# Every third lower weight part of the second block's projections, made by GpSimd

## The chip, the cores and the metric

The kernel runs on one core of one Trainium2 chip. The metric is the device time of one execution in microseconds (us). The core has five engines that each work through their own instructions in a fixed order: TensorE (PE in the rows; its weight loads are PEld), VectorE (DVE), ScalarE (ACT), GpSimd (POOL) and SyncE (SP, which issues the DMAs here). Engines wait for one another through semaphores. An instruction that waits holds up all that stand behind it on its engine.

## The reference

Two different transformer blocks run one after the other on 256 tokens of width 1024. The second one, cut to the part that matters here:

```python
c_q, c_kv, k_pe, dq, dk, dv = split(h @ w_in, [384, 256, 32, 512, 512, 512])
# _mla: 8 heads of 96 columns, the last 32 of them with rotary positions
q  = _rms(c_q, cq_g) @ w_uq
kv = _rms(c_kv, ckv_g) @ w_ukv              # 64 key and 64 value columns per head
q, k = _rms(q, q_g), _rms(concat(k_nope, k_pe), k_g)
o_mla = softmax(mask(q @ k.T * scale)) @ v
# _diff_attn: 4 heads, each with two softmaxes that are subtracted
o_diff = _rms((p1 - lam * p2) @ dv, subln_g) * (1.0 - lambda_init)
x = x + g1 * (concat(o_mla, o_diff) @ w_o)
x = x + g2 * _hmoe(h2, ...)                 # router and 16 experts
```

Everything is fp32. The first block (two feed-forward parts, token mixing, a per-layer embedding) and the experts of the second one are the larger share of the time. The change leaves both as they are.

## The kernel before

**Products.** TensorE multiplies in a reduced fp32 format, so every fp32 operand is split into an upper part `whi` and a lower part `wlo`, and a product takes three matmuls (`mm3`, L332 to L334). `split` (L336) makes the two parts: ScalarE copies the raw weights into the reduced format (L337), VectorE subtracts that from the raw weights (L338). The two lines are also used for activations (`xTh`, `xTl`, `cqTh`, `cqTl`).

**Pieces.** `piece` (L262) loads one piece of a weight matrix, at most 128 x 2048, with one DMA (L265) into a raw tile and cuts it into parts, of 128 x 512 as a rule, each with one split. There are three raw tiles in the stages spoken of here (`wraw`), which rotate: the DMA of a piece has to wait until all splits of the piece three before it have read their raw tile. SyncE issues these DMAs in program order, so one that waits holds back those behind it.

**The second block's projections.** `attention2` runs `mla_project` and `diff_project` interleaved. After the norm in front (around 1180 to 1200 us of the span) come, in the order of their DMAs: two pieces of the columns 0 to 672 of `w_in` (`lat`, the low-rank inputs), the V columns of `w_in`, `w_uq` in two pieces (queries, `mla_q`), `w_ukv` in two pieces (keys and values, `mla_k`), the columns 672 to 1696 of `w_in` in four pieces (`diff_q`, `diff_k`), and `w_o` in four pieces. For each query half and token tile there is a chain: matmuls into a bank `pj`, squares and sums (`gr_sq` L1338, `gr_ss` L1340), a reciprocal root (`rs_m`, `gr_rs`, L387 to L394), scaling (`mla_q` L1418, `mla_k` L1443), four transposes by TensorE (L1424, L1448) into `pt`, and a copy by ScalarE into `mla_qT` (L1428). Then scores and softmax follow (`mla_s` L1477).

**GpSimd** makes masks and position tables at the start. In the second block it only fills the two extra rows of the key and query tiles with mask constants: 16 instructions of 2 partitions for `mla_kT` (L1409) and 4 for `mla_qT` (L1427).

**Order.** A tile framework orders the instructions of each engine when the program is built, by priorities, and places the waits; the order is fixed when the program runs.

Of the kernel before, what the change touches and what calls it, by code (L numbers as in the profile page):

```python
# [8 lines left out]
F32 = mybir.dt.float32  # L9
# [3 lines left out]
ALU = mybir.AluOpType  # L13
# [39 lines left out]
class Net:  # L53
# [7 lines left out]
    hold = None  # L61
    first = ()
    log_behind = None

    def __init__(self, tc, ctx, a):
        self.tc, self.ctx, self.a = tc, ctx, a
        self.nc = tc.nc
        pool = lambda name, bufs, **kw: ctx.enter_context(tc.tile_pool(name=name, bufs=bufs, **kw))
        self.const = pool("const", 1)
        self.act = pool("act", 2)  # L70
        self.wraw = pool("wraw", 3)
        self.wspl = pool("wspl", 8)
        self.ring = pool("ring", 11)
        self.gring = pool("gring", 16)
        self.cring = pool("cring", 6)
        self.tmp = pool("tmp", 12)
        self.ps = pool("ps", 3, space=PSUM)
        self.psc = pool("psc", 3, space=PSUM)
        self.pst = pool("pst", 2, space=PSUM)
        self.tacts = []  # L80
        self.ada_part = []
        self.act_set(SILU_SET)
        self.masks()
# [172 lines left out]
    def piece(self, src, kk, n, by=0):  # L256

        nc = self.nc
        m = kk * n
        raw = self.raw()  # L260
        rv = raw[:, :m].rearrange("p (k n) -> p k n", k=kk)
        n0 = 0  # L262
        for z in src if isinstance(src, tuple) else (src,):
            n1 = n0 + z.shape[1]
            nc.sync.dma_start(out=rv[:, :, n0:n1], in_=z.rearrange("(k p) n -> p k n", p=P))  # L265
            n0 = n1
        k2, n2 = (min(kk, 1024 // n), n) if by == 0 else (kk, min(n, 1024 // kk))
        k2 = -(-kk // -(-kk // k2))
        out = []
        for k0 in range(0, kk, k2):  # L270
            for n0 in range(0, n, n2):
                h = rv[:, k0:min(k0 + k2, kk), n0:n0 + n2]
                w = h.shape[1]
                hi = self.wspl.tile([P, 1024], F32R, name="whi")[:, :w * n2].rearrange("p (k n) -> p k n", k=w)
                lo = self.wspl.tile([P, 1024], F32R, name="wlo")[:, :w * n2].rearrange("p (k n) -> p k n", k=w)
                cuts = [slice(None)]
                if w * n2 > 512 and (self.raws is None or self.raws <= 3):
                    cuts = [slice(0, w // 2), slice(w // 2, w)] if w > 1 else cuts
                for k in cuts:
                    ends = self.split(hi[:, k], lo[:, k], h[:, k])  # L280
                    for ins, o in zip(ends, self.before_weights):
                        self.after(ins, o)
                    if self.hold is not None:
                        self.after(ends[1], self.hold)
                    for ins, o in zip(ends, self.first):
                        self.after(ins, o)
                out.append((hi, lo))
        self.before_weights = ()
        return out
# [43 lines left out]
        mm(out, l[0], r[1], start=False, stop=False)  # L333
        mm(out, l[1], r[0], start=False, stop=stop)  # L334

    def split(self, hi, lo, src):  # L336
        h = self.split_hi = self.nc.scalar.activation(hi, src, AF.Copy).ins  # L337
        self.mark = self.nc.vector.tensor_tensor(lo, src, hi.bitcast(F32), ALU.subtract).ins  # L338
        return h, self.mark

# [1311 lines left out]
    def attention2(self):  # L1652
        nc, a = self.nc, self.a
        if self.depth == 0 or "p" not in self.stages:
            self.weave([self.attention_in(t) for t in range(NT)], 1)
        self.xT = self.hT
        oT = self.new_xT()
        m, d = self.mla_project(), self.diff_project()
        for n, z in enumerate((m, d, m, m)):
            self.weave(next(z))  # L1660
            if n == 1:
                self.first = ()
        mla = self.mla_attend(oT)
        self.weave(mla[0] + mla[1], 3)
        self.weave(next(d))
        diff = self.diff_attend(oT)
        self.weave(diff[0] + diff[1], 2)
        self.router_tables()
        self.router_weights()
        g1 = self.gate_row(0)  # L1670
        self.logits, self.xs, self.rt_rstd = {}, {}, {}
        self.rt_lg = self.c([P, NT, 20], "logits")
        w, o = a["w_o_2"][0], {}
        hs = lambda h: slice(h * 512, h * 512 + 512)
        pcs = {(h, k0): self.piece_k(w[k0 * P:k0 * P + 512, hs(h)], 4, 512) for k0 in (0, 4) for h in range(2)}

        def products(t, h, k0):

            if k0 == 0:
                o[t, h] = (self.ch_bank if t and h else self.mm_bank)("wo")  # L1680
            tt = slice(t * P, t * P + P)
            for k in range(k0, k0 + 4):
                self.mm3(o[t, h], (oT[0][:, k, tt], oT[1][:, k, tt]), pcs[h, k0][k - k0], k == 0, k == KD - 1)

        def finish(t, h):
            products(t, h, 4)
            r = self.s("wo_r")
            nc.vector.tensor_tensor(r, o[t, h], g1[h], ALU.mult)
            xs = self.x[:, t, hs(h)]
            self.summed = nc.vector.tensor_tensor(xs, xs, r, ALU.add).ins  # L1690
            self.router_in(t, h)
            if h == 1:
                rstd = self.rt_rstd[t] = self.c([P, 1], f"rt_rstd{t}")
                self.weave([self.rstd(rstd, self.mean_square(t), D)])
                nc.vector.scalar_tensor_tensor(self.rt_lg[:, t], self.logits[t][:, :20], rstd, self.rt_b, ALU.mult, ALU.add)
                self.tokens(t)

        for t, h in ((0, 0), (0, 1), (1, 0)):
            products(t, h, 0)
        finish(0, 0)  # L1700
        products(1, 1, 0)
        finish(0, 1)
        finish(1, 0)
        finish(1, 1)
# [239 lines left out]
    def moe(self):  # L1944
        nc, a = self.nc, self.a
        self.router()

        self.raws = 0

        def in_act():  # L1950
            z = self.new_xT()
            return lambda k: tuple(y[:, k:k + 2] for y in z)
        in_g = lambda k: tuple(self.g(n, F32R).rearrange("p (k n) -> p k n", k=2) for n in ("moe_xh", "moe_xl"))
        pair = lambda g, new: self.gather(2, lambda t: self.r1[:, t, g:g + 2], new)
        tiles = pair(0, in_act())
        self.act_set(SILU_SET, self.split_hi)
        self.g2 = self.gate_row(1)
        self.expert_tiles(tiles, [lambda name, e, g=g: a[name][0, g * E_PER_G + e] for g in range(N_GROUPS)], lambda: pair(2, in_g))

        v = nc.vector  # L1960
        info = self.c([1, 2], "over_f")
        ov = self.c([1, 4], "over_o")
        idx = self.c([1, 4], "over_i")
        for j in range(4):
            nc.gpsimd.memset(idx[:, j:j + 1], float(j * E_PER_G))
        v.tensor_reduce(info[:, 0:1], self.count[0:1], AX.X, ALU.max)
        v.tensor_scalar(ov, self.count[0:1], float(P), None, ALU.is_gt)
        v.tensor_tensor(ov, ov, idx, ALU.mult)
        v.tensor_reduce(info[:, 1:2], ov, AX.X, ALU.add)
        ii = self.c([1, 2], "over_ii", I32)  # L1970
        v.tensor_copy(ii, info)
        rr = self.c([P, NT], "over_r")
        v.tensor_reduce(rr, self.r1, AX.X, ALU.max)
        v.tensor_scalar(rr, rr, float(P), None, ALU.subtract)
        n = nc.values_load(ii[0:1, 0:1], min_val=0, max_val=S)
        e0 = nc.values_load(ii[0:1, 1:2], min_val=0, max_val=12)
        with self.tc.If(n > P):
            tiles = self.gather(1, lambda t: rr[:, t:t + 1], in_act())
            self.expert_tiles(tiles, [lambda name, e: a[name][0, bass.ds(e0 + e, 1)].rearrange("o k n -> (o k) n")])
# [85 lines left out]
```

## Time and profile before

| | |
|---|---|
| runs | 1656.74 us median of 3 (1653.23 to 1657.44) |
| profiled execution, its own time | 1653.4 us |
| its span | 1651.7 us, so 1.7 us lie around the span |
| PE busy | 1610.7 us (98%) |
| DVE busy | 1285.3 us (78%) |
| ACT busy | 896.4 us (54%) |
| POOL busy | 26.2 us (2%) |
| mean granted TensorE clock | 0.991 |

Times of single instructions below are microseconds from the start of the span. A busy share says how much of a stretch an engine had an instruction running, not how well it ran. The stage of the change lies between about 1180 and 1345 us; before it is the first block, after it the experts.

### The profile page before, as it was taken

To read this page: it belongs to the slowest core of one execution; us is meant where nothing else is said; L and a number is where in the kernel's file an instruction comes from. 1 tells how busy PE (TensorE), PEld (TensorE's weight loads), DVE (VectorE), ACT (ScalarE), POOL (GpSimd) and SP (SyncE) were. 2 spreads that over 40 slices of the span, in tenths; PEclk is the share of its full clock that TensorE was granted. 3 is DMA by queue.
4 is the path that set the end of the run, shared out by engine and by line. 5 is a ranking of instruction groups with operands and counts; after the bars stand their busy time and mean duration, and the time that the engine had idled before them with its cause. 6 is when DMAs were issued, how large, how long until landed. Compare 5 with 4: busy or idle time off the path is not lost.

```text
span 1651.7 us, 24570 instructions
## 1 busy us (share of the span) xinstructions
PE 1610.7 (98%) x9269; PEld 1344.7 (81%) x9269; DVE 1285.3 (78%) x2395; ACT 896.4 (54%) x1599; POOL 26.2 (2%) x90
## 2 busy tenths in 40 slices
PE   8999999999999999999999999999889999999998
PEld 6888898888888878888988888888778778787876
DVE  7668878577669886688885686697877769999896
ACT  6544365454553445544563645534475567777674
POOL 2000000000000000000000000000200000000000
PEclk9999999999999999999999999999999999999998
DMA  8667662236568756577532455676343239899995
GB/s 293 212 204 252 201 183 78 99 134 209 192 215 275 242 162 204 184 255 243 179 104 77 161 182 183 221 279 218 120 159 104 101 124 375 299 349 325 360 343 193
DMA packets 175261, 342.46 MB, mean 207 GB/s; under 512 B 13033, under 2 KB 49954, under 8 KB 175138
## 3 DMA queue, kind: packets, MB, share of 16 engines
q1 hardware_dynamic: 175138, 340.84, 60.4%
q8 instruction: 75, 1.23, 0.3%
q14 instruction: 48, 0.39, 0.1%
HBM read 339.76 MB, written 1.05 MB: 206 GB/s over the span
## 4 chain that ended last, share of the span: by engine, by line
PE 84%; DVE 9%; ACT 3%; DMA 2%; issue 1%; SPq 0%; DVEq 0%; ACTq 0%
PE gu L332 9%; PE gu L333 9%; PE gu L334 9%; PE pT L576 6%; PE y L334 4%; PE y L333 4%; PE y L332 4%; PE moe_h L333 4%; PE moe_h L334 3%; PE moe_h L332 3%; DVE wlo L338 2%; PE sc L576 2%; PE moe_y L333 2%; PE moe_y L332 2%; PE moe_y L334 2%; PE pj L332 2%
## 5 line engine op out<-in xcount | busy, mean ns | idle before, releaser
L338 DVE TENSOR_TENSOR wlo<-wraw,whi 128x512 fp32r<-128x512 f32 (+2 forms) x758 | 605.6, 831 | 157.2 <-ACT whi L337 155.0
L337 ACT ACTIVATE whi<-wraw 128x512 fp32r<-128x512 f32 (+2 forms) x758 | 528.3, 741 | 363.8 <-issue 104.2
L332 PE MATMUL gu<-whi,xTh 128*128 128x512 f32 (+1 forms) x736 | 274.9, 373 | 0.0
L333 PE MATMUL gu<-wlo,xTh 128*128 128x512 f32 (+1 forms) x736 | 274.1, 372 | 0.0
L334 PE MATMUL gu<-whi,xTl 128*128 128x512 f32 (+1 forms) x736 | 273.7, 372 | 0.0
L334 PEld LDWEIGHTS gu<-whi,xTl 128*128 128x128 f32 x736 | 138.8, 189 | 23.2
L332 PEld LDWEIGHTS gu<-whi,xTh 128*128 128x128 f32 x736 | 138.7, 188 | 23.1
L333 PEld LDWEIGHTS gu<-wlo,xTh 128*128 128x128 f32 x736 | 138.8, 189 | 22.7
L332 PE MATMUL y<-whi,hTh 128*128 128x512 f32 x224 | 87.7, 391 | 0.0
L334 PE MATMUL y<-whi,hTl 128*128 128x512 f32 x224 | 87.6, 391 | 0.0
L333 PE MATMUL y<-wlo,hTh 128*128 128x512 f32 x224 | 87.3, 390 | 0.2 <-DVE wlo L338 0.2
L332 PE MATMUL y<-whi,xTh 128*128 128x512 f32 x192 | 75.7, 394 | 0.0
L576 PE MATMUL pT<-xTh,whi 128*128 128x256 f32 x256 | 75.7, 296 | 0.0
L333 PE MATMUL y<-wlo,xTh 128*128 128x512 f32 x192 | 75.0, 391 | 0.0
L576 PE MATMUL pT<-xTl,whi 128*128 128x256 f32 x256 | 75.0, 293 | 0.0
L334 PE MATMUL y<-whi,xTl 128*128 128x512 f32 x192 | 75.0, 391 | 0.0
L576 PE MATMUL pT<-xTh,wlo 128*128 128x256 f32 x256 | 74.4, 291 | 0.0
L1166 DVE SCALAR_TENSOR_TENSOR ada<-ada_w,silu_c,ada 128x512 f32<-128x512 f32 x84 | 62.7, 746 | 12.7 <-DMA ada_w<-in_w_ada_dram 12.3
L1279 DVE SCALAR_TENSOR_TENSOR bias<-rel_m,rel_delta,bias 128x384 f32<-128x384 bf16 x116 | 63.9, 612 | 0.5
L109 ACT ACTIVATE ffn_h<-gu 128x512 f32<-128x512 f32 (+1 forms) x48 | 27.0, 563 | 55.4 <-PE gu L334 55.4
L337 ACT ACTIVATE xTh<-pt 128x512 fp32r<-128x512 f32 (+1 forms) x72 | 35.6, 500 | 35.1 <-PE pt L355 29.6
L333 PE MATMUL moe_h<-wlo,moe_xh 128*128 128x512 f32 x128 | 50.8, 397 | 1.7 <-DVE wlo L338 1.7
(570 smaller groups left out, 3254.6 us busy)
## 6 DMA issues: line engine op xcount, KB each, us to landing
wraw<-in_ffn_w_in_dram SPq DMA_DIRECT2D x88, 1024.0 KB
wraw<-in_ffn_w_out_dram SPq DMA_DIRECT2D x44, 1024.0 KB
wraw<-in_mix_w_in_dram SPq DMA_DIRECT2D x26, 1024.0 KB
ada_w<-in_w_ada_dram SPq DMA_DIRECT2D x96, 256.0 KB
wraw<-in_w_gate_dram SPq DMA_DIRECT2D x20, 1024.0 KB
wraw<-in_w_up_dram SPq DMA_DIRECT2D x19, 1024.0 KB
wraw<-in_w_down_dram SPq DMA_DIRECT2D x19, 1024.0 KB
wraw<-in_mix_w_out_dram SPq DMA_DIRECT2D x8, 1024.0 KB
```

The source lines that it names most:

```text
L109: ins = self.nc.scalar.activation(*args, **kw).ins
L332: mm(out, l[0], r[0], start=start, stop=False)
L333: mm(out, l[0], r[1], start=False, stop=False)
L334: mm(out, l[1], r[0], start=False, stop=stop)
L337: h = self.split_hi = self.nc.scalar.activation(hi, src, AF.Copy).ins
L338: self.mark = self.nc.vector.tensor_tensor(lo, src, hi.bitcast(F32), ALU.subtract).ins
L576: self.nc.tensor.matmul(o[:, :S], w[:, k], z[:, k], start=k == 0 and n == 0, stop=k == KD - 1 and n == 2)
L1166: z = nc.vector.scalar_tensor_tensor(acc, raw, c, acc, ALU.mult, ALU.add)
L1279: z = nc.vector.scalar_tensor_tensor(b, m, d, b, ALU.mult, ALU.add)
```

## The change

`piece` counts its splits (`turn`). While `share` is 3, every third split has its subtraction issued on GpSimd instead of VectorE. `share` is set to 3 in `attention2` ahead of the projections and back to 0 in front of the experts. The upper part stays on ScalarE. The other splits stay as they are. `mark`, which other code uses to put filler work behind the last subtraction, is not set by a GpSimd one.

```diff
     first = ()
     log_behind = None
+    turn = 0
+    share = 0
 ...
                 for k in cuts:
-                    ends = self.split(hi[:, k], lo[:, k], h[:, k])
+                    self.turn += 1
+                    ends = self.split(hi[:, k], lo[:, k], h[:, k], self.share and self.turn % self.share == 0)
 ...
-    def split(self, hi, lo, src):
+    def split(self, hi, lo, src, other=False):
+
         h = self.split_hi = self.nc.scalar.activation(hi, src, AF.Copy).ins
+        if other:
+            return h, self.nc.gpsimd.tensor_tensor(lo, src, hi.bitcast(F32), ALU.subtract).ins
         self.mark = self.nc.vector.tensor_tensor(lo, src, hi.bitcast(F32), ALU.subtract).ins
         return h, self.mark
 ...
         oT = self.new_xT()
+        self.share = 3
         m, d = self.mla_project(), self.diff_project()
 ...
         self.raws = 0
+        self.share = 0
```

What it does to the order of the instructions can be seen on three engines. Names with the same number are the same tile in both. Line numbers shift by a few: L265 becomes L267, L337 becomes L341, and those from L1224 on by six (L1409 becomes L1415, L1427 becomes L1433, L1428 becomes L1434, L1338 becomes L1344); GpSimd's subtraction is L343.

GpSimd from the last position table to the first instruction of the router, before:

```order
L1249 TENSOR_TENSOR rel_i_622<-pos_r_618,pos_nq_620 128x128
L1250 TENSOR_TENSOR rel_i_622<-pos_r_618,pos_nq_620 128x256
L1409 TENSOR_SCALAR mla_kT_11982<-early_137 2x2x64 x4
L1409 TENSOR_SCALAR mla_kT_11983<-early_137 2x2x64 x4
L1409 TENSOR_SCALAR mla_kT_11984<-early_137 2x2x64 x4
L1409 TENSOR_SCALAR mla_kT_11985<-early_137 2x2x64 x4
L1427 COPY mla_qT_12184<-early_137 2x512
L1427 COPY mla_qT_12187<-early_137 2x512
L1427 COPY mla_qT_12190<-early_137 2x512
L1427 COPY mla_qT_12193<-early_137 2x512
L1810 IOTA iota1i_12947 128x128
```

and now, from the last of the early subtractions on (11949 is of the V columns, 12006 and 12038 are `w_uq`, 12220 the second piece of `w_ukv`, 12498 and 12536 the first two pieces of the `diff` columns):

```order
L343 TENSOR_TENSOR wlo_11949<-wraw_11940,whi_11948 128x512
L343 TENSOR_TENSOR wlo_12015<-wraw_12006,whi_12014 128x384
L343 TENSOR_TENSOR wlo_12047<-wraw_12038,whi_12046 128x384
L343 TENSOR_TENSOR wlo_12223<-wraw_12220,whi_12222 128x512
L1415 TENSOR_SCALAR mla_kT_11982<-early_137 2x2x64 x4
L1415 TENSOR_SCALAR mla_kT_11983<-early_137 2x2x64 x4
L1415 TENSOR_SCALAR mla_kT_11984<-early_137 2x2x64 x4
L1415 TENSOR_SCALAR mla_kT_11985<-early_137 2x2x64 x4
L1433 COPY mla_qT_12184<-early_137 2x512
L1433 COPY mla_qT_12187<-early_137 2x512
L1433 COPY mla_qT_12190<-early_137 2x512
L1433 COPY mla_qT_12193<-early_137 2x512
...
L343 TENSOR_TENSOR wlo_12501<-wraw_12498,whi_12500 128x512
```

GpSimd has 19 subtractions more: 8 stand ahead of its twenty fills, 11 behind them (5 of the `diff` columns, 6 of `w_o`). Before, the fills stood behind nothing but the tables made at the start.

SyncE at the DMAs of the `diff` columns and the first two of `w_o`, with the engines that each waits for, before:

```order
L265 DMA wraw_12498<-in_w_in_2_dram 128x4x512 [waits DMAHW7_49,DVE_49]
L265 DMA wraw_12536<-in_w_in_2_dram 128x4x512 [waits DMAHW0_49,DVE_49,Activation_49]
L265 DMA wraw_12576<-in_w_in_2_dram 128x4x512 [waits DMAHW1_49,DVE_49,Activation_49]
L265 DMA wraw_12614<-in_w_in_2_dram 128x4x512 [waits DMAHW2_49,DVE_49,Activation_49]
L265 DMA wraw_12989<-in_w_o_2_dram 128x4x512 [waits DMAHW3_49,DVE_49]
```

and now:

```order
L267 DMA wraw_12498<-in_w_in_2_dram 128x4x512 [waits DMAHW7_49,DVE_49,Pool_49]
L267 DMA wraw_12536<-in_w_in_2_dram 128x4x512 [waits DMAHW0_49,DVE_49,Activation_49]
L267 DMA wraw_12576<-in_w_in_2_dram 128x4x512 [waits DVE_49,DMAHW1_49,Activation_49,Pool_49]
L267 DMA wraw_12614<-in_w_in_2_dram 128x4x512 [waits DVE_49,DMAHW2_49,Activation_49,Pool_49]
L267 DMA wraw_12989<-in_w_o_2_dram 128x4x512 [waits DMAHW3_49,DVE_49,Pool_49]
```

The order of the DMAs is the same. The fourth piece of the `diff` columns (12614) goes into the raw tile of the first one (12498), so it now waits for the subtraction `wlo_12501`, which stands behind all the fills on GpSimd.

ScalarE around the upper parts of that fourth piece, now:

```order
L341 ACTIVATE whi_12584<-wraw_12576 128x512 x2
L1434 ACTIVATE mla_qT_12184<-pt_12164,cols2_577 96x512
L341 ACTIVATE whi_12616<-wraw_12614 128x512 x2
L341 ACTIVATE whi_12622<-wraw_12614 128x512
L1434 ACTIVATE mla_qT_12187<-pt_12169,cols2_577 96x512
L341 ACTIVATE whi_12622<-wraw_12614 128x512
L1434 ACTIVATE mla_qT_12190<-pt_12174,cols2_577 96x512
L1344 ACTIVATE gr_sq_12242<-pj_12196 128x256
L1344 ACTIVATE gr_sq_12246<-pj_12197 128x256
L1344 ACTIVATE gr_sq_12250<-pj_12218 128x256
```

Before, the first upper part of 12614 stood ahead of `mla_qT_12184` and the other three between that and `mla_qT_12187`. The squares `gr_sq` begin the chain of the keys: their tile `pj_12196` is the first product with `w_ukv`. They stand behind all four upper parts of 12614.

## Rows read from the trace of the kernel before

**Rows 1.** The page: engines, and the chain that ended last, by engine.
```profile
PE 1610.7 (98%) x9269; PEld 1344.7 (81%) x9269; DVE 1285.3 (78%) x2395; ACT 896.4 (54%) x1599; POOL 26.2 (2%) x90
...
PE 84%; DVE 9%; ACT 3%; DMA 2%; issue 1%; SPq 0%; DVEq 0%; ACTq 0%
```

**Rows 2.** Stretch, its length, busy us of PE, PEld, DVE, ACT, POOL; clock, DMA share, GB/s.
```profile
1228.50:1246.30 17.80, 13.83 (x65) 10.11 (x64) 17.80 (x88) 13.14 (x41) 0.00 (x0) 1.00 0.60 193
1246.30:1281.00 34.70, 34.70 (x208) 29.26 (x208) 24.88 (x50) 19.74 (x59) 0.00 (x0) 1.00 0.33 106
```

**Rows 3.** Waits from 1228.5 to 1246.5: total us, times, longest us.
```profile
PE pj L332 <- DVE mla_q L1418: 2.1, 2, 1.3
...
PE pj L332 <- DVE rs_m L393: 1.6, 1, 1.6
```

**Rows 4.** GpSimd's groups in the whole span: busy us, mean ns, idle before.
```profile
L1427 POOL COPY mla_qT<-early 2x512 f32<-2x512 f32 x4 | 2.3, 613 | 17.6 <-PE pj L333 17.6
L1250 POOL TENSOR_TENSOR rel_i<-pos_r,pos_nq 128x256 int32<-128x256 int32 x1 | 0.6, 611 | 0.0
...
L204 POOL TENSOR_TENSOR m16f<-s,m4f 128x128 f32<-128x128 f32 x1 | 0.5, 452 | 0.1
...
L1249 POOL TENSOR_TENSOR rel_i<-pos_r,pos_nq 128x128 int32<-128x128 int32 x1 | 0.4, 398 | 38.1 <-DMA pos_r<-in_positions_dram 38.1
```

**Rows 5.** Timeline of GpSimd, 1165 to 1345: start, length, instructions, idle before.
```profile
1170.14 5.22 POOL L1409 TENSOR_SCALAR mla_kT<-early 2x128 f32<-2x128 f32 x8 [1118.79 <-DVE ln_r L417]
1185.60 7.63 POOL L1409 TENSOR_SCALAR mla_kT<-early 2x128 f32<-2x128 f32 x8 [10.23 <-ACT rms_h L1321]
1210.87 2.29 POOL L1427 COPY mla_qT<-early 2x512 f32<-2x512 f32 x4 [17.64 <-PE pj L333]
```

**Rows 6.** Timeline of SyncE's DMA issues, 1212 to 1240.
```profile
1217.38 14.14 SPq L265 DMA_DIRECT2D wraw<-in_w_in_dram  x4
1236.56 0.37 SPq L265 DMA_DIRECT2D wraw<-in_w_o_dram  x1
```

**Rows 7.** Timeline of ScalarE, 1218 to 1223, 1235 to 1243 and 1262 to 1272.
```profile
1220.98 1.67 ACT L337 ACTIVATE whi<-wraw 128x512 fp32r<-128x512 f32 x3
...
1236.46 0.63 ACT L337 ACTIVATE whi<-wraw 128x512 fp32r<-128x512 f32 x1 [1.66 <-DMA wraw<-in_w_in_dram]
...
1237.57 1.66 ACT L337 ACTIVATE whi<-wraw 128x512 fp32r<-128x512 f32 x3
1239.13 0.67 ACT L1428 ACTIVATE mla_qT<-pt,cols 96x512 f32<-96x512 f32 x1
...
1241.53 1.18 ACT L1338 ACTIVATE gr_sq<-pj 128x256 f32<-128x256 f32 x4
...
1268.80 1.15 ACT L337 ACTIVATE whi<-wraw 128x512 fp32r<-128x512 f32 x2 [2.69 <-PE pj L334]
```

**Rows 8.** Timeline of VectorE: around 1187, and 1221 to 1232.
```profile
1187.54 1.29 DVE L338 TENSOR_TENSOR xTl<-rms_h,xTh 128x512 fp32r<-128x512 f32 x2
...
1225.28 0.55 DVE L1340 TENSOR_REDUCE gr_ss<-gr_sq 128x4 f32<-128x384 f32 x1
...
1230.41 1.29 DVE L338 TENSOR_TENSOR wlo<-wraw,whi 128x512 fp32r<-128x512 f32 x2
```

**Rows 9.** Timeline of TensorE: first product with the `diff` columns, first transpose of keys.
```profile
1239.77 0.47 PE L332 MATMUL pj<-whi,xTh 128*128 128x512 f32 x1 [1.26 <-DVE mla_q L1418]
...
1246.38 0.61 PE L1448 MATMUL pt<-ident,mla_k 128*96 128x128 f32 x4
```

**Rows 10.** Timeline of GpSimd in two short windows, 1186.7 to 1187.5 and from 1190.5.
```profile
1186.19 3.02 POOL L1409 TENSOR_SCALAR mla_kT<-early 2x128 f32<-2x128 f32 x2
...
1190.54 0.53 POOL L1409 TENSOR_SCALAR mla_kT<-early 2x128 f32<-2x128 f32 x1
```

**Rows 11.** Busy time by stretch around TensorE's wait for the norm; columns as in rows 2.
```profile
1187.50:1192.50 5.00, 5.00 (x16) 5.00 (x17) 5.00 (x12) 3.91 (x6) 4.71 (x5) 0.50 0.00 0
1192.50:1203.00 10.50, 10.50 (x58) 9.31 (x58) 9.49 (x29) 4.36 (x10) 0.70 (x1) 0.98 0.64 213
```

## Prediction

> **What bounds the kernel now.** The page first [rows 1]: TensorE is busy for 98% of the span and holds 84% of the chain that ended last, so VectorE, though busy for 78%, is worth something only where TensorE waits for it. GpSimd, with 2%, looks free. These are averages, though, and the change touches only one stage, so next the busy time by stretch [rows 2]. From 1228.5 to 1246.3 VectorE is busy for all 17.8 us and TensorE for 13.83: here VectorE is the bound. From 1246.3 to 1281 TensorE is busy for all 34.7 us: what is late at 1246.3 is late for good. The waits of the first of these stretches [rows 3] say what there is to win: TensorE waits 2.1 + 1.6 = 3.7 us for VectorE's normalization of the queries. Last, I follow the engine that gets the work: when GpSimd is at its old work, how long that takes, and which transfers its results release.
>
> **The change, part by part.** 19 subtractions leave VectorE, 19 go to GpSimd. In the order shown ahead, 8 of them stand before GpSimd's twenty fills, 11 behind them. Their upper parts stay on ScalarE.
>
> *One subtraction on GpSimd.* The trace has none of 128x512. Two inputs of 128x128 fp32 took 0.452 us; the integer form took 0.398 at 128 columns and 0.611 at 256 [rows 4], so 0.213 more for 128 columns. 0.452 + 3 x 0.213 = 1.09: I take 1.1 us, an estimate from these rows, against about 0.65 on VectorE (two in 1.29) [rows 8]. One price is so near the other that it decides nothing.
>
> *The eight early ones* (two of the low-rank inputs, three V, two `w_uq`, one `w_ukv`). GpSimd was idle for most of 1193 to 1226 [rows 5], so they cost nothing by their length; TensorE has other products to run there. What they change is the start of the fills. Before, these ran at 1170.14 and 1185.60, far ahead of need [rows 5]. Now all sixteen stand behind the subtraction of the second `w_ukv` piece, whose upper part is the second of three from 1220.98 on and ends near 1222.1 [rows 7]. From 1222 to 1225.28 VectorE runs subtractions and small products of two inputs back to back, up to the reduction at 1225.28 [rows 8]. In such a run before, one fill that takes 0.53 us was stretched: two took 3.02 us around 1187.54 [rows 8, 10]. So GpSimd gets through at 1225.3, and with 1.1 us is done at 1226.4; without that block, 1222.1 + 1.1 = 1223.2.
>
> *The fills, in their new place.* The first eight took 5.22 us (0.65 each), the second eight 7.63 us (0.95 each) [rows 5]. The second eight ran beside a VectorE that was busy for 5.00 of 5.00 us [rows 11]; the new place has 17.80 of 17.80 [rows 2]. So I take 0.95: 16 x 0.954 = 15.3 us, with 10.4 as the other bound. Four query fills took 2.29 us [rows 5]. Then comes the first `diff` subtraction, 1.1 us: done at 1226.4 + 15.3 + 2.3 + 1.1 = **1245.1**.
>
> The Trainium skill states a rule for this, on the page "SBUF — State Buffer", section "Who interferes with whom": a VectorE instruction with two SBUF inputs contends with a GpSimd instruction that reads SBUF, and the one that issues second is blocked until the first finishes. The stretched fill [rows 10] agrees for GpSimd as the one that waits; the other direction no row here shows, and it is a rival below.
>
> *The transfer behind it.* The fourth `diff` piece takes the raw tile of the first and now waits for GpSimd. SyncE's four issues lasted from 1217.38 to 1231.52 [rows 6]; the last one, 0.37 us as the next [rows 6], began at 1231.16, right after the last VectorE subtraction of the first piece, in the pair of 1230.41 [rows 8]. The issue now comes at 1245.2, **14.0 us later**. From issue to ScalarE's first upper part were 1236.46 − 1231.16 = 5.3 us [rows 6, 7]: data at 1250.5.
>
> *What is queued behind it.* ScalarE's four upper parts of this piece stand ahead of the squares that begin the keys. Four parts at 0.53 (three in 1.66, less overlap) and two query copies at about 0.6 [rows 7] make 3.3 us: squares at 1253.8 instead of 1241.53, **12.3 us later**. From squares to TensorE's first key transpose were 1246.38 − 1241.53 = 4.85 us [rows 7, 9], which stay: 1258.7 instead of 1246.38.
>
> *TensorE meanwhile.* The first `diff` product began at 1239.77 [rows 9]; it now stops at the lower part from GpSimd until 1245.1. The 24 matmuls of the first piece that TensorE has in front of the key transposes need some 5.6 us at 0.23 us spacing, so it is through near 1251, before 1258.7: that wait is hidden by the later one. A wait of TensorE may cost clock: after the one at the norm the granted clock was 0.50, its level of 1.2 GHz, for 5 us, then 0.98 [rows 11]. Bounds 0 and 2.5 us, from the same rows; I take 1.
>
> *What is won.* The 3.7 us of [rows 3] lie ahead of the new stop, so TensorE only reaches it earlier: 0. Later, in the `diff` queries, the lighter VectorE may give 0.5 us.
>
> *Edits that cost nothing.* The `w_o` transfers follow on SyncE, the first 8 to 14 us later than 1236.56 [rows 6], but its upper parts were made at 1268.80 [rows 7], 32 us after the issue: covered. If that cover were gone, it would be the same 12 us, not more. `share` back at 0 leaves the experts as they were, all shifted.
>
> *Sum.* +12.3 + 1 − 0.5 = +12.8; I count 1.5 less, since VectorE has four subtractions fewer in front of the fills' stretch and stalls itself once the squares are late, which lets GpSimd pass: **+11.3**. On the profiled execution 1653.4 + 11.3 = 1664.7. The median of the runs is 1656.74, 3.3 above it, and a new median is compared with that: **1668**.
>
> **The rivals.**
>
> *Same: GpSimd keeps up.* Without any block the first `diff` subtraction ends at 1223.2 + 10.4 + 2.3 + 1.1 = 1237.0, the data come at 1242.4, the squares at 1245.7: +4.2, so 1661. For it: the first eight fills ran at 0.65 us. Against it: VectorE is full here [rows 2]. It decides at 1238: ending before that, the loss is under 5 us.
>
> *Faster: the relief counts.* If the fills were through in time, the 3.7 us of waits could go, and 0.5 later: 1652.5. ScalarE had 1236.46 + 3.3 = 1239.8 against 1241.53, some 1.8 us to spare, so the first subtraction must end by 1232.9. That leaves 6.3 us for sixteen fills, 0.39 each; no row has one under 0.53 [rows 10].
>
> *Slower still: GpSimd also holds VectorE.* By the rule named above a subtraction on GpSimd would hold VectorE's two-input instructions for its 1.1 us. As a mechanism of this kernel: the three `diff` subtractions that fall between the squares and the keys add 3 x 1.1 = 3.3 us to the 4.85, so +12.3 + 3.3 + 1 = +16.6: 1673. For it: VectorE's work there is two-input chains. Against it: at 1187.54, the two subtractions kept their 0.65 us each [rows 8] beside a waiting fill.
>
> **How the numbers follow.** Forecast 0.60; rival with both engines held 0.18; GpSimd keeps up 0.18; faster 0.04. A measurement of this kernel tells about 0.3%, 5 us, from no change. Faster by more than that: 0.03, of the 0.04 of the relief, which lands near the bound. Within: 0.18, the rest of that and the keeping up, less 0.01 that comes out above 5 us. Slower: 0.79, the two remaining cases and that 0.01. The fills' bounds (10.4 to 15.3, with or without 3.2 of block) and the clock reach from 1660 to 1670, the holding to 1673 and, with 2.5 of clock and another 2 us of blocked fills, to 1677. The range is 1657 to 1676.
>
> **What the changed profile would show.** GpSimd's fills in one row from about 1226, over 12 us long, and the subtractions after them from about 1244; SyncE's fourth `diff` issue there; ScalarE idle for some 10 us before an upper part, released by that DMA, where it had 1.66; the first key transpose near 1258. In the stretch after it TensorE full for 34.7 us as before. Wrong would be: fills that end before 1234, a fourth issue before 1238, or key squares that don't wait for that transfer.

## The result, and the profile after

The changed kernel takes 1666.84 us (median of 4 runs, 1661.03 to 1667.41) against 1657.05 for the kernel before (4 runs): a ratio of 1.0061, 95% interval 1.0043 to 1.0079, so 10 us slower, between 7 and 13. The forecast was 1668, slower. The profiled execution of the change took 1661.03 us, its span 1659.3; it is the shortest of its four runs, as the profiled one before (1653.4) lies near the shortest of its.

The page, engines and chain, of the kernel after [rows 1]:

```profile
PE 1611.7 (97%) x9269; PEld 1344.5 (81%) x9269; DVE 1288.3 (78%) x2376; ACT 896.7 (54%) x1599; POOL 52.8 (3%) x109
...
PE 86%; DVE 9%; ACT 3%; DMA 1%; issue 1%; SPq 0%; DVEq 0%; ACTq 0%
```

Nineteen instructions left VectorE, and it is busy for 3 us *longer* than before. That is the first sign of what happened. GpSimd took 26.6 us more.

The two profiled executions don't run level when they come to the stage: the first low-rank product is at 1184.44 after and was at 1187.47 before, so 3.0 us must be added to times of after before they are held against those of before. These 3 us come from before the stage, in work that the change leaves alone. The row before, and the row after:

```profile
1187.47 0.69 PE L332 MATMUL pj<-ghi,xTh 128*128 128x384 f32 x1 [4.76 <-ACT xTh L337]
```

```profile
1184.44 0.69 PE L335 MATMUL pj<-ghi,xTh 128*128 128x384 f32 x1 [5.01 <-ACT xTh L341]
```

Busy time by stretch, after; the first two rows answer to [rows 2]. Each of these ends at the same instruction as there: the first at the first key transpose, the second 34.7 us later.

```profile
1225.50:1251.80 26.30, 17.24 (x69) 12.51 (x68) 23.84 (x88) 13.32 (x41) 17.68 (x19) 0.81 0.54 188
1251.80:1286.50 34.70, 34.68 (x208) 29.21 (x208) 23.37 (x42) 19.97 (x59) 5.43 (x5) 1.00 0.26 81
...
1238.00:1246.50 8.50, 4.47 (x14) 3.40 (x15) 7.74 (x23) 3.92 (x9) 5.77 (x4) 0.50 0.86 272
```

The first stretch grew from 17.8 to 26.3 us, with a count of 88 VectorE instructions in both, but 23.84 us of VectorE instead of 17.80. TensorE's granted clock fell from 1.00 to 0.81; the third row lies in the part of the stretch in which it was at 0.50, the level of 1.2 GHz. The second one is full for TensorE, as before. So the loss arises in front of the key transposes and isn't made up.

GpSimd's timeline over that stretch, after:

```profile
1219.19 1.48 POOL L343 TENSOR_TENSOR wlo<-wraw,whi 128x512 fp32r<-128x512 f32 x1 [4.38 <-ACT whi L341]
1220.76 12.44 POOL L1415 TENSOR_SCALAR mla_kT<-early 2x128 f32<-2x128 f32 x16
1233.24 2.83 POOL L1433 COPY mla_qT<-early 2x512 f32<-2x512 f32 x4
1236.16 4.92 POOL L343 TENSOR_TENSOR wlo<-wraw,whi 128x512 fp32r<-128x512 f32 x4
1243.81 2.79 POOL L343 TENSOR_TENSOR wlo<-wraw,whi 128x512 fp32r<-128x512 f32 x1 [2.73 <-ACT whi L341]
```

The queue is the one forecast: fills behind the `w_ukv` subtraction, query copies, then the `diff` subtractions, four of them in one row by now, since their upper parts had long been there.

SyncE's fourth `diff` issue and ScalarE behind it, after [rows 6, 7]:

```profile
1237.45 0.37 SPq L267 DMA_DIRECT2D wraw<-in_w_in_dram  x1
```

```profile
1242.58 1.67 ACT L341 ACTIVATE whi<-wraw 128x512 fp32r<-128x512 f32 x3 [7.20 <-DMA wraw<-in_w_in_dram]
...
1245.82 1.18 ACT L1344 ACTIVATE gr_sq<-pj 128x256 f32<-128x256 f32 x4
...
1248.58 0.68 ACT L1434 ACTIVATE mla_qT<-pt,cols 96x512 f32<-96x512 f32 x1 [1.05 <-PE pt L1430]
```

With the 3.0 us, the transfer is issued at 1240.4 instead of 1231.16, and the key squares come at 1248.8 instead of 1241.53.

Now what the forecast had not on the path. VectorE's timeline beside the `w_ukv` subtraction (the first row) and beside the four `diff` subtractions (1236.16 to 1241.08), after:

```profile
1219.44 1.27 DVE L1376 TENSOR_TENSOR rope_u<-kpe_r,cos 128x16 f32<-128x16 f32 x1
...
1235.52 0.63 DVE L1376 TENSOR_TENSOR rope_u<-mla_q,cos 128x64 f32<-128x64 f32 x1
1236.07 0.21 DVE L1377 TENSOR_TENSOR rope_u<-mla_q,cos 128x64 f32<-128x64 f32 x1
1236.21 1.29 DVE L1378 TENSOR_TENSOR rope_w<-mla_q,sin 128x64 f32<-128x64 f32 x1
1237.42 1.30 DVE L1379 TENSOR_TENSOR rope_w<-mla_q,sin 128x64 f32<-128x64 f32 x1
1238.64 0.54 DVE L1424 TENSOR_TENSOR mla_q<-pj,gr_rs 128x384 f32<-128x384 f32 x1
1239.11 0.83 DVE L1380 TENSOR_TENSOR mla_q<-rope_u,rope_w 128x64 f32<-128x64 f32 x1
1239.87 1.30 DVE L1381 TENSOR_TENSOR mla_q<-rope_u,rope_w 128x64 f32<-128x64 f32 x1
```

A rotary step on 64 columns takes 0.21 us; beside a GpSimd subtraction it takes 1.29 or 1.30, so it is stopped for about 1.07 (the one at 1235.52 is still beside the query copies). The multiplication `mla_q<-pj,gr_rs`, whose first input is a matmul result, keeps its 0.54. TensorE's waits in the stretch, and the transposes that waited, after [rows 3]:

```profile
PE pt L1430 <- DVE mla_q L1381: 5.6, 1, 5.6
...
PE pj L335 <- DVE mla_q L1424: 3.4, 3, 1.5
```

```profile
1241.22 1.09 PE L1430 MATMUL pt<-ident,mla_q 128*96 128x128 f32 x4 [5.63 <-DVE mla_q L1381]
1243.12 0.76 PE L335 MATMUL pj<-whi,xTh 128*128 128x512 f32 x1 [0.82 <-DVE mla_q L1424]
...
1251.58 0.39 PE L337 MATMUL pj<-whi,xTl 128*128 128x512 f32 x1
1251.82 0.39 PE L1454 MATMUL pt<-ident,mla_k 128*96 128x128 f32 x2
```

TensorE waits 5.63 us for the last of those rotary steps. It then works through the `diff` products, with one more wait of 0.82 us, and comes to the key transposes at 1251.82 without waiting for them: the keys were ready at 1251.7. Two late paths end at the same place, as they did before (keys at 1246.2, transposes at 1246.38).

The two are not independent. The reciprocal roots of the keys (`rs_y`) stand on ScalarE behind the fourth query copy. That is the last row of ScalarE above: the squares are made, and ScalarE waits 1.05 us for TensorE's fourth query transpose. VectorE waits for the roots:

```profile
1250.21 0.35 DVE L398 TENSOR_TENSOR gr_rs<-rs_y 128x4 f32<-128x4 f32 x3 [1.20 <-ACT rs_y L111]
```

So in this execution the late queries hold the keys as well, and the late transfer had about 1 us to spare. The 8.5 us that are lost up to the key transposes fall into two parts. TensorE begins the `diff` products at 1246.1 by the clock of before instead of 1239.77 [rows 9], 6.4 us later. From there it needs 8.70 us instead of 6.61 for the same 24 products and 8 query transposes: up to 2.1 us are the half clock.

### The profile page after: what moved, and what is told of

Same layout as the page of the kernel before. It is cut to its first block, busy times and chain, and to the rows that moved or that the text cites. A ratio compares the mean times of both kernels' runs of the same rounds, so it can differ in the third digit from the quotient of the medians.

```text
span 1659.3 us, 24601 instructions
## 1 busy us (share of the span) xinstructions
PE 1611.7 (97%) x9269; PEld 1344.5 (81%) x9269; DVE 1288.3 (78%) x2376; ACT 896.7 (54%) x1599; POOL 52.8 (3%) x109
## 3 DMA queue, kind: packets, MB, share of 16 engines
q8 instruction: 75, 1.23, 0.3%
HBM read 339.76 MB, written 1.05 MB: 205 GB/s over the span
## 4 chain that ended last, share of the span: by engine, by line
PE 86%; DVE 9%; ACT 3%; DMA 1%; issue 1%; SPq 0%; DVEq 0%; ACTq 0%
PE gu L335 9%; PE gu L337 9%; PE gu L336 9%; PE pT L582 6%; PE y L337 5%; PE y L336 5%; PE y L335 5%; PE moe_h L336 3%; PE moe_h L337 3%; PE moe_h L335 3%; DVE wlo L344 2%; PE sc L582 2%; PE moe_y L335 2%; PE moe_y L336 2%; PE moe_y L337 2%; PE pj L335 2%
## 5 line engine op out<-in xcount | busy, mean ns | idle before, releaser
L341 ACT ACTIVATE whi<-wraw 128x512 fp32r<-128x512 f32 (+2 forms) x758 | 528.6, 741 | 376.8 <-issue 107.2
L344 DVE TENSOR_TENSOR wlo<-wraw,whi 128x512 fp32r<-128x512 f32 (+2 forms) x739 | 596.9, 838 | 160.2 <-ACT whi L341 157.9
L337 PE MATMUL gu<-whi,xTl 128*128 128x512 f32 (+1 forms) x736 | 273.8, 373 | 0.0
L337 PEld LDWEIGHTS gu<-whi,xTl 128*128 128x128 f32 x736 | 138.6, 188 | 23.1
L337 PE MATMUL y<-whi,hTl 128*128 128x512 f32 x224 | 87.6, 391 | 0.0
L337 PE MATMUL y<-whi,xTl 128*128 128x512 f32 x192 | 75.0, 391 | 0.0
L343 POOL TENSOR_TENSOR wlo<-wraw,whi 128x512 fp32r<-128x512 f32 (+3 forms) x19 | 26.6, 1406 | 1197.6 <-ACT whi L341 1196.3
L341 ACT ACTIVATE xTh<-pt 128x512 fp32r<-128x512 f32 (+1 forms) x72 | 35.6, 500 | 34.8 <-PE pt L361 29.7
```

The costliest lines, as they stand in the source:

```text
L343: return h, self.nc.gpsimd.tensor_tensor(lo, src, hi.bitcast(F32), ALU.subtract).ins
```

## The experiments

All times are of the whole kernel, differences against the kernel before on the same chip, 95% intervals in brackets. Each is worked out from the recorded ratio of the two, so it can lie 1 or 2 us off a difference of medians. In most kernels one number of the trace serves beside the time: the stretch from the first query product to the first key transpose, 24.15 us before, and VectorE's **held time** in it (over all VectorE instructions that overlap one of GpSimd, the time that each took beyond the median length of the same form in the kernel before).

**1. Only the first eight subtractions.** Every third cut is counted, and only the listed ones are made by GpSimd (the same edit, with other lists, serves for four more runs).

```diff
+    nth = 0
+    on_pool = (1, 2, 3, 4, 5, 6, 7, 8)
 ...
         if other:
+            self.nth += 1
+        if other and self.nth in self.on_pool:
             return h, self.nc.gpsimd.tensor_tensor(lo, src, hi.bitcast(F32), ALU.subtract).ins
```

> Only the first 8 of the 19 subtractions stay on GpSimd (low-rank inputs, V, w_uq, second w_ukv piece), the 11 of the diff columns and of w_o are back on VectorE. The sixteen fills are as late as in the change. Transfer theory (the loss is the fourth diff transfer, held back by a GpSimd subtraction behind the fills): that transfer waits for VectorE again and is issued at most 1 us later than before relative to the stage's start; 0 to +2 us in all. Hold theory (the loss is GpSimd's subtractions of the diff columns holding VectorE's query chain): these are gone too, 0 to +2 us. If the late fills by themselves cost VectorE time, 3 us or more.

Measured: +6.1 us [3.0, 9.4]. More than both theories allowed, and what the last sentence has for the late fills: with no `diff` or `w_o` subtraction on GpSimd, and the fourth transfer on time, over half of the loss is there.

**2. Only the last eleven**, list 9 to 19.

> Only the last 11 subtractions stay on GpSimd (5 of the diff columns, 6 of w_o); the first 8 are on VectorE, so the fills run early as before and GpSimd is free when the diff columns come. Transfer theory: the fourth diff transfer is issued within 2 us of before, so the loss up to the first key transpose goes, and at most what w_o costs is left: 0 to +3 us. Hold theory: five subtractions of 1.26 us still stand beside VectorE's saturated query chain, 5 x (1.26 - 0.65) = 3 us or more are lost there, and w_o costs the same as in the change: +4 to +8 us.

Measured: +5.1 us [2.8, 7.5]; in the trace GpSimd's fills run early again, and the fourth issue comes 0.6 us earlier than before within SyncE's four (13.52 us for the four against 14.14). The transfer is on time, and half of the loss is there as well. The hold theory is the one that said so.

**3. All but the one that the transfer waits for**, list without 9.

> The change with one subtraction put back on VectorE: that of the first diff piece, for which the fourth transfer waits. 18 stay on GpSimd. Transfer theory: the fourth transfer is on time, and most of the +8.6 us at the first key transpose goes; +1 to +4 us in all with what w_o costs. Hold theory: the three next subtractions still run in one row behind the fills and hold VectorE's rotary steps for 3 x 1.26 us, TensorE waits some 4 us for the queries as before it waited 5.6, and the clock falls: +6 to +10 us in all.

Measured: +9.3 us [6.6, 11.9]. SyncE, GpSimd and VectorE of this kernel, and TensorE's wait:

```profile
1222.52 13.96 SPq L269 DMA_DIRECT2D wraw<-in_w_in_dram  x4
```

```profile
1243.69 5.25 POOL L347 TENSOR_TENSOR wlo<-wraw,whi 128x512 fp32r<-128x512 f32 x4
```

```profile
1244.07 1.28 DVE L1380 TENSOR_TENSOR rope_u<-mla_q,cos 128x64 f32<-128x64 f32 x1
1245.28 1.30 DVE L1381 TENSOR_TENSOR rope_u<-mla_q,cos 128x64 f32<-128x64 f32 x1
1246.50 1.30 DVE L1382 TENSOR_TENSOR rope_w<-mla_q,sin 128x64 f32<-128x64 f32 x1
1247.72 1.30 DVE L1383 TENSOR_TENSOR rope_w<-mla_q,sin 128x64 f32<-128x64 f32 x1
```

```profile
1249.81 0.45 PE L1434 MATMUL pt<-ident,mla_q 128*96 128x128 f32 x1 [5.66 <-DVE mla_q L1385]
```

The four issues take 13.96 us as before (14.14, [rows 6]), so the transfer of the forecast is mended, and nothing comes back. Four rotary steps are stopped again, and TensorE's wait is 5.66 us where the change has 5.63. ScalarE makes the key squares no earlier, though all upper parts are there: they stand behind a query copy that waits for TensorE.

```profile
1253.80 0.68 ACT L1438 ACTIVATE mla_qT<-pt,cols 96x512 f32<-96x512 f32 x1 [2.18 <-PE pt L1434]
1254.38 1.18 ACT L1348 ACTIVATE gr_sq<-pj 128x256 f32<-128x256 f32 x4
```

Counted from the first query product the squares come after 27.5 us, where the change has 26.6 and the kernel before 19.3.

**4. The late transfer without `diff` subtractions.** As run 1, and a GpSimd copy of one element makes the fourth transfer wait for the fills (`last_fill` is the last of the four query copies).

```diff
+            if self.nth == 9:
+                t = self.nc.gpsimd.tensor_copy(self.c([P, 1], "tie")[0:1], src[0:1].rearrange("p k n -> p (k n)")[:, 0:1]).ins
+                self.after(t, self.last_fill)
 ...
```

> As the run with only the first 8 subtractions, and beside it one GpSimd copy of a single element of the first diff piece's raw tile, put behind the fills. It makes the fourth transfer wait as in the change, with no subtraction of GpSimd beside the query chain. The copy's result is not used. Transfer theory: issue some 5 to 6 us later than before, squares of the keys 3 to 5 us later, first key transpose 3 to 5 us later: +3 to +6 us. Hold theory: TensorE's long wait for the queries is gone, and the keys alone cost less than that: 0 to +2 us.

Measured: +6.6 us [3.5, 9.6], where run 1 had +6.1: the late transfer adds 0.5 us, with some 4 us of uncertainty either way. In its one profiled execution it is not free: the stretch is 32.67 us instead of 28.91 in run 1, and TensorE waits 2.48 us for a ScalarE copy that stood behind the transfer's upper parts (the order on ScalarE differs by one copy from the change there). So a late transfer can cost by itself; the times are too wide to show that it does.

**5. The key fills put into a gap, with the first eight subtractions.** `last_fill` is the last of the sixteen key fills here.

```diff
             z = self.nc.gpsimd.tensor_tensor(lo, src, hi.bitcast(F32), ALU.subtract).ins
+            if self.nth == 6:
+                self.after(z, self.last_fill)
 ...
```

> As the run with only the first 8 subtractions, with GpSimd's sixteen key fills put ahead of the two w_uq subtractions, where GpSimd was idle. In that run nothing of the diff columns or of w_o was on GpSimd and yet 6 us were lost; TensorE waited 2.99 us once for the queries and its clock fell to 0.50 behind that. Theory 1 (the late fills, with the copies, slow VectorE's query chain): the wait shrinks to 2 us or less, the clock stays at 1.00, and the time is within 2 us of before. Theory 2 (the subtraction of the second w_ukv piece holds VectorE for 1.1 us and that is enough): wait and clock stay, +4 to +7 us.

Measured: +1.8 us [-0.8, 4.5]. The stretch is back at 24.43 us, held time 0.74, TensorE's clock at 1.00 in it. Theory 1 holds: with the fills in the gap 4.3 of run 1's 6.1 us are gone. Something else moved with them. The four `diff` transfers are issued 3 to 8 us later here, counted from the first query product (the fourth at 16.2 us instead of 8.9), and ScalarE makes the upper parts of the fourth behind the key squares, so the keys don't wait for it.

**6. Late fills alone**, all subtractions on VectorE.

```diff
+            if self.nth == 8:
+                t = self.nc.gpsimd.tensor_copy(self.c([P, 1], "tie")[0:1], hi[0:1].bitcast(F32).rearrange("p k n -> p (k n)")[:, 0:1]).ins
+                for f in self.fills:
+                    self.after(f, t)
 ...
```

> The kernel before with no subtraction on GpSimd, and the twenty fills held back behind one GpSimd copy of a single element of the upper part of the second w_ukv piece, so that they run from about 1222 us on as in the change; the copy's result is not used. Theory 1 (late fills slow VectorE): VectorE's instructions beside the fills take some 2.5 us more in all, TensorE waits longer than 2 us for the queries, and the clock falls: +4 to +6 us. Theory 2 (it takes a subtraction): 0 to +2 us.

Measured: +2.5 us [0.2, 5.0], under theory 1's 4 to 6, and the clock did fall (0.50 at 1240 to 1245). The held time is 2.63 us, as expected, and the stretch is 2.8 us longer. VectorE beside the four query copies, in this kernel:

```profile
1238.42 0.63 DVE L1385 TENSOR_TENSOR rope_u<-mla_q,cos 128x64 f32<-128x64 f32 x1
1238.97 0.63 DVE L1386 TENSOR_TENSOR rope_u<-mla_q,cos 128x64 f32<-128x64 f32 x1
1239.52 0.64 DVE L1387 TENSOR_TENSOR rope_w<-mla_q,sin 128x64 f32<-128x64 f32 x1
1240.08 0.63 DVE L1388 TENSOR_TENSOR rope_w<-mla_q,sin 128x64 f32<-128x64 f32 x1
```

A copy of 512 columns on two partitions stops a rotary step for 0.41 us: these fills, which were free where they stood, cost where they now stand.

**7. Is it the clock?** As run 1, with more work for TensorE in front of its long wait.

```diff
-                for k in range(k0, k1):
-                    self.mm3(acc[t][:, :n], lhs(k, tt), pc[k - k0], k == 0, k == K - 1)
+                for _ in range(1 + (redo if t == NT - 1 else 0)):
+                    for k in range(k0, k1):
+                        self.mm3(acc[t][:, :n], lhs(k, tt), pc[k - k0], k == 0, k == K - 1)
 ...
-            return self.proj(a["w_ukv_2"][0][:, half * 512:half * 512 + 512], 512, use, K=2,
+            return self.proj(a["w_ukv_2"][0][:, half * 512:half * 512 + 512], 512, use, K=2, redo=2 * (half == 0),
```

> As the run with only the first 8 subtractions, and TensorE does the product of the first w_ukv piece with the second token tile three times instead of once (12 matmuls, 2.8 us more), just ahead of its wait of 2.99 us; the last one counts. Clock theory (the 6 us are mostly the half clock that follows the wait): the wait is filled, the clock stays at 1.00 up to the keys, and the time falls to +0 to +2 us, though TensorE does more. If the loss is the late queries themselves, the extra work changes nothing or costs up to 1 us: +5 to +7 us.

Measured: +6.1 us [3.5, 8.9], the same as run 1. Busy time by stretch around the wait, of run 1 and of this run:

```profile
1235.00:1250.00 15.00, 10.74 (x36) 8.06 (x37) 14.26 (x54) 9.12 (x25) 6.06 (x10) 0.66 0.48 162
```

```profile
1230.00:1250.00 20.00, 15.58 (x73) 11.81 (x72) 20.00 (x86) 12.90 (x41) 8.36 (x13) 1.00 0.63 216
```

The clock stayed at 1.00 instead of 0.66, the first wait shrank from 2.99 to 0.28 us, and the next one grew to 2.62. The stretch is 28.00 us instead of 28.91. So the clock theory falls for run 1: the first `diff` product starts 21.40 us into the stretch at half clock and 21.38 at full clock, where TensorE waits for VectorE's queries instead. What the half clock adds comes behind that, 0.9 us.

**8. Only `w_o`**, list 14 to 19.

> Only the six subtractions of w_o stay on GpSimd. Each holds VectorE by up to 1.1 us around the diff queries; in the profiles with them TensorE waits 2.58 us there instead of 1.17. Without a fall of the clock: +1 to +2 us; with one behind that wait, as in the profile of the change: +3 us. If the w_o part is free, 0.

Measured: +1.0 us [-1.5, 3.5]: not told from nothing. VectorE is held for 4.14 us here too, all of it behind the stretch, and TensorE waits 2.58 us for the `diff` queries, as in the change, instead of 1.17. So in the trace 4.14 us of held time away from the bound cost 1.4 us of wait.

**9. All nineteen, with the key fills in the gap** (the edit of run 5).

> The change with all 19 subtractions, and the sixteen key fills put ahead of the two w_uq subtractions, where GpSimd was idle. Nothing late stands ahead of the diff subtractions any more, and the fourth diff transfer is on time. Hold theory (each GpSimd instruction that reads on-chip memory stops VectorE's two-input instructions for its length, and counts where VectorE is the bound): the holds by the late fills and query copies go, some 2.5 to 3 us, those of the diff subtractions stay: +5 to +8 us. Transfer theory: the queue and the transfer are mended, +0 to +3 us.

Measured: +7.6 us [5.0, 10.4], 2.5 less than the change, with intervals that overlap. The queue is mended. The fourth transfer is not on time, as the expectation had it: it is issued 16.3 us after the first query product (before 8.9, in the change 18.2). But as in run 5 its upper parts stand behind the key squares, so the keys don't wait for it. Three quarters of the loss stay.

**10. Only the `diff` columns**, list 9 to 13, fills early.

> Only the five subtractions of the diff columns on GpSimd, fills early as before. Hold theory: four of them fall into the stretch in which VectorE is the bound, 4 x (1.07 held - 0.6 of own work saved) = 2 us at least, and as the held instructions stand in the query chain up to 4.3 us: +2 to +5 us. If w_o made the loss of the run with both: 0 to +1 us.

Measured: +4.6 us [2.2, 7.0]; held time 4.46 us, and the stretch 4.24 us longer. The five subtractions that were to relieve VectorE lengthen its chain by what they hold it. That the lower parts come later from GpSimd is not the cause: neither here nor in the change does a wait of TensorE in this stage end with a GpSimd subtraction.

**11. Reads alone.** The kernel before, with GpSimd copies that nobody uses.

```diff
+            if self.nth in (9, 10, 11, 12):
+                self.scr = self.scr or self.c([P, P], "scr")
+                for n in range(3):
+                    self.nc.gpsimd.tensor_copy(self.scr, hi.bitcast(F32).rearrange("p k n -> p (k n)")[:, n * P:n * P + P])
```

> The kernel before, all subtractions on VectorE, and behind the upper parts of four diff parts three GpSimd copies of 128x128 each into a scratch tile that nobody reads (about 0.3 us each, 12 in all). Hold theory: GpSimd's reads alone stop VectorE, 12 x some 0.25 us = 3 us in the query chain: +2 to +4 us, VectorE's held time in the profile 2.5 us or more. If it is the place of the subtraction in the data flow that costs (lower part late for TensorE, later transfers): 0.

Measured: +2.3 us [-0.2, 4.6], not told from nothing, and the trace doesn't have the expected reason: VectorE was held for 0.63 us in all, not 2.5. GpSimd's timeline of this run:

```profile
1226.80 2.52 POOL L350 COPY scr<-whi 128x128 f32<-128x128 f32 x3 [12.57 <-ACT whi L344]
1231.50 3.70 POOL L350 COPY scr<-whi 128x128 f32<-128x128 f32 x6 [2.18 <-ACT whi L344]
1235.38 1.52 POOL L350 COPY scr<-whi 128x128 f32<-128x128 f32 x3 [0.18 <-ACT whi L344]
```

The copies took 0.84, 0.62 and 0.51 us each in the three groups: of like instructions the first take half as long again as the last, so here GpSimd is mostly the one that waits. This run is inconclusive in time and a miss for the size of my expectation.

**12. Writes alone**, the copies of run 11 replaced by one of 128x1 and five fills with a constant.

```diff
+                self.nc.gpsimd.tensor_copy(self.scr[:, 0:1], hi.bitcast(F32).rearrange("p k n -> p (k n)")[:, 0:1])
+                for n in range(5):
+                    self.nc.gpsimd.memset(self.scr, 0.0)
```

> As the run with GpSimd copies, with the copies replaced by one copy of 128x1 and five fills with a constant of 128x128 (about 0.2 us each, 20 in all), which read nothing. Hold theory in the form that only GpSimd's reads stop VectorE: 0 to +1 us, held time under 1 us. If any GpSimd instruction stops it: +2 to +4 us as with the copies.

Measured: -1.7 us [-4.1, 0.7], no difference. Held time 0.00, though twenty fills ran beside a full VectorE:

```profile
1231.02 1.27 POOL L351 MEMSET scr<- 128x128 f32 x5
...
1235.71 1.26 POOL L351 MEMSET scr<- 128x128 f32 x5
```

Each fill took 0.21 us, as long as the like ones of the kernel before (0.206): neither engine waits for the other. The four copies of one column in front of them, which read, took 1.36, 1.38, 0.50 and 0.19 us.

**Held time against the stretch**, one profiled execution each, from the traces; the last column is the time of the whole kernel:

```
GpSimd makes                       held us   stretch us (before 24.15)   whole kernel
nothing, writes only (12)             0.00     24.17   +0.0                 -1.7
w_o (8)                               0.00     24.27   +0.1                 +1.0
nothing, short reads (11)             0.63     25.28   +1.1                 +2.3
first eight, fills in the gap (5)     0.74     24.43   +0.3                 +1.8
nothing, late fills (6)               2.63     26.96   +2.8                 +2.5
first eight, late fills (1)           3.75     28.91   +4.8                 +6.1
diff columns and w_o (2)              4.12     27.96   +3.8                 +5.1
diff columns (10)                     4.46     28.39   +4.2                 +4.6
all, fills in the gap (9)             5.59     29.32   +5.2                 +7.6
all, the change                       7.39     32.62   +8.5                +10.1
all but one, transfer on time (3)     7.60     33.20   +9.1                 +9.3
first eight, late transfer (4)        3.73     32.67   +8.5                 +6.6
```

Run 7 is left out, since it adds work to TensorE in the stretch. Apart from the last row, the stretch grows by what VectorE is held, within 1.5 us. No version here is clearly faster than the kernel before.

## Why the prediction was right, and where it was not

The direction, the place and the size were right: slower by 10 where 11.3 was forecast, lost in front of the key transposes and not made up in the full stretch behind them. The mechanism was right only in part, and the rival with the chance of 0.18 has the better half of the case. That the number came so near is luck in part: the path that was added up was sized some 4 us too long, and the loss came by another one. None of the three signs of being wrong showed either; they tested whether the transfer is late, not whether it sets the end.

- *One subtraction on GpSimd*, 1.1 us: four in a row took 4.92, 1.23 each. Near enough for the queue.
- *The start of the fills.* 1226.4 was forecast; with the 3.0 us it was 1223.8. VectorE's run did not keep the `w_ukv` subtraction out: that got in near the run's start, at 1219.19, and stopped a rotary step of 0.17 us for 1.1. The step "so GpSimd gets through at 1225.3" failed: it got in behind the one VectorE subtraction that was running (1218.97 to 1219.52) and held the next instruction, where the fill of [rows 10] had waited for three more behind it. No run shows what decides that.
- *The fills*, 15.3 us: 12.44, 0.78 each, near the mean of the two rows in [rows 5] (0.80) and not their slower half. Query copies 2.83 instead of 2.3. The first `diff` subtraction ends at 1240.4 by the clock of before, not 1245.1.
- *The transfer and what is queued behind it.* Issue 9.3 us later instead of 14.0, squares 7.3 us later instead of 12.3. The chain was as described down to the squares. From squares to key transposes it took 6.0 us, not the 4.85 "which stay": ScalarE's fourth query copy stands in between and waited for TensorE. So the key transposes came 8.5 us later than before (12.3 forecast).
- *That this chain sets the end.* This is the step that failed: run 3 takes the transfer's wait away, and +9.3 us stay. "That wait is hidden by the later one", said of TensorE's wait for the `diff` products, had the right idea and the wrong wait: TensorE stood still for 5.63 us at the query transposes, which the working had as unchanged, and from there on it was 10.6 us to the key transposes. The keys hang on the same queries, by the query copies on ScalarE.
- *What is won*, "0": it was less than that. The subtractions that left VectorE were 0.65 us each of filling in between, and each one came back as up to 1.07 us of a stop in the query chain. The relief of 3.7 us [rows 3] turned into 9.0 us of waits.
- *The clock*, 1 us: the fall was there (0.50 from 1237.7 to 1247.9). Run 7 shows for run 1 that it costs 0.9 us of the stretch. In the change it is at most 2.1 us, the 8.70 instead of 6.61 behind the first `diff` product; no run takes the clock alone there.
- *The 1.5 us taken off the sum* rest on no row. What ran shorter than counted was the fills, by 2.9 us.
- *Edits that cost nothing.* `w_o` was counted as covered by its transfers' slack, which it is. Its subtractions hold VectorE for 4.1 us, at a measured +1.0, not told from nothing.

The rival "GpSimd also holds VectorE" was priced for three subtractions between squares and keys, +3.3 on top of the late transfer. The mechanism is real, its place was one stage earlier, at the queries, and it stands beside the transfer, not on top of it. Where the rival looked for it, it can be seen in run 9: a `diff` subtraction at 1251.87 stops a step of the keys' roots, which takes 1.14 us instead of 0.15, and TensorE waits 1.57 us for the keys. Against it stood the row at 1187.54, where two VectorE subtractions kept their 0.65 us beside a waiting fill [rows 8, 10]. That row shows a GpSimd fill of 128 columns that came second. It says nothing on a GpSimd subtraction of 512 columns with two inputs that comes first, and I read it as if it did.

The Trainium skill's rule, "SBUF — State Buffer", section "Who interferes with whom", was the better guide here. It says that whichever of a two-input VectorE instruction and a reading GpSimd instruction issues first keeps the other out, and that a GpSimd instruction that only writes doesn't contend. The traces agree with both directions: a fill stretched by VectorE at 1187, rotary steps of 0.21 us stretched to 1.30 by GpSimd, and none by the twenty writes of run 12.

What stays open: what the late transfer alone would cost in the change. Run 4's times say 0.5 us, its one profile says 3.8, and its order on ScalarE is not quite that of the change. What is shown is that the loss is the same without it, and that in the change's own trace it had about 1 us to spare.

## What to carry to other kernels

Work moved to an idle engine is only free if the two engines don't stop each other: here a subtraction of 0.65 us on VectorE became one of 1.25 us on GpSimd that stopped VectorE for up to 1.07, so each one moved beside such work made the bound engine slower. Before moving work to GpSimd beside a full VectorE, count the two-input VectorE instructions that will run next to it, and look where GpSimd's old work ends up behind the new in its queue. And where two late paths join, look whether one hangs on the other, and mend one on the chip before believing that it is the one that counts.

## What the runs showed of the hardware

- A GpSimd subtraction of 128x512 with two inputs stopped a two-input VectorE instruction for up to 1.11 us (about 1.07 for most rotary steps, 0.3 to 0.7 for many subtractions), a one-input copy of 512 columns on two partitions for 0.41, fills from a row of 128 columns and copies of 128x128 for 0.08 to 0.11 each, writes of a constant not at all. The number of partitions did not matter in these rows, the columns read did.
- VectorE's multiplication with one input from a matmul result kept its 0.54 us beside a GpSimd subtraction.
- Where VectorE comes first, GpSimd waits: the fifth `diff` subtraction took 2.79 us instead of 1.26.
- In run 1 a half clock of TensorE over some 10 us cost 0.9 us: at full clock (run 7) it waits for VectorE instead and starts the `diff` products no earlier.
